# A DRAM-to-DRAM cast of two row tiles, issued per row tile instead of for both at once

## The chip, the core and the metric

The kernel runs on one core of a Trainium2 chip. The metric is the device time of one execution in microseconds (us). A core has TensorE (PE in the profile; PEld is its weight load), VectorE (DVE), ScalarE (ACT), GpSimd (POOL) and SyncE (SP), which work side by side and wait for each other through semaphores, and 16 DMA engines that move data when POOL or SP issues a transfer.

## The reference

```python
# a: 1024 x 4096 float32, b: 4096 x 4096 float32
x = np.matmul(a, b)
return special.logsumexp(x, axis=-1)      # 1024 values
```

## The kernel before

**Tiling.** Rows of `a` are split into 8 row tiles m of 128 (row p*8 + m stands in tile m), the inner dimension k into 32 tiles of 128, the columns of `b` into 8 blocks `nb` of 512. TensorE works in float16; the DMAs that POOL issues cast from float32 to float16 on the way. TensorE needs `a` transposed, and the tile `aT` holds it so for the whole run.

**Seven products instead of eight.** Two row tiles make a pair q (tiles 2q and 2q+1; q = 0 to 3), two k tiles a pair i (16 of them), and a block of 512 columns is two halves of 256. Each q and block is then a 2x2 block product, done with seven products m1 to m7 of 16 matmuls each (128x128 by 128x256) rather than eight. For that VectorE makes sums and differences: of `aT` the tiles `s1`, `s2`, `s5` (`a_sums_early`) and two differences in place (`a_sums_late`), and of each block of `b` the tiles T1, T4, T6 (in `tb`) and two more in place (`make`). The order of the products of one q is m1, m5, m2, m6, m3, m4, m7; ScalarE copies results out of PSUM between them, VectorE adds them up and takes row maxima, ScalarE sums exponentials.

**Stages.** In the first 65 us row tiles 0 to 5 come in, are transposed on TensorE and multiplied plainly with block 0. Then `plan` gives the steps: step 0 is block 1 with q = 0, 1, 2 worked jointly; steps 1 to 6 are blocks 2 to 7 with q = 0 to 3; the last two steps do q = 3 for blocks 0 and 1. PSUM tiles are named acc_q_h (h = 0 or 1, with a running number behind), so acc_2_0_1475 belongs to q = 2 of step 1 and acc_3_0_1608 to q = 3 of step 1. Columns of `b` are in tiles b_0 to b_3, one for each quarter of k, again with a running number: 744 to 747 are block 2 (used in step 1), 1205 to 1208 are block 3 (used in step 2).

**Row tiles 6 and 7** (q = 3) take another way, in step 0 (L356 to L365). For each half h of k (2048 columns), POOL issues a DMA that casts both row tiles from `a` to a float16 tile in DRAM, `a16_h` (2 x 128 x 2048; the profile names the two a_0_752 and a_1_756). Then SP issues two transposing DMAs from `a16_h` into `aT`, one for each row tile. VectorE makes the sums of q = 3 for the lower half of k behind q = 1 of step 1 (L529 to L531) and for the upper half in q = 2 of step 1, ahead of m3 (L503 to L505). q = 3 of step 1 is their first user.

**Order.** Each engine works its own instructions strictly in the order of the program (`manual_schedule`). POOL's order around the casts is: four loads of block 2, the casts, two loads of block 3, then a one-row copy into `ident` (L349) that reads what the first pair of transposes wrote and so holds POOL until they have landed, then the other two loads of block 3.

Of the kernel before, what the change touches and what calls it, by code (L numbers as in the profile page):

```python
# [13 lines left out]
def kernel(  # L14
# [6 lines left out]
    nc = tc.nc  # L21
# [12 lines left out]
    MT, KT, NB = M // P, K // P, N // FD  # L34
# [5 lines left out]
    a_m = a.rearrange("(p mt) k -> mt p k", mt=MT)  # L40
# [295 lines left out]
    for step, (_, qs) in enumerate(plan):  # L336
# [4 lines left out]
        if more:  # L341
            if plan[step + 1][0] is again1:
                nxt = last
            else:
                nxt = plan[step + 1][0]()
                if step == 1:
# [3 lines left out]
                        out=ident[0:1, 0:2], in_=aT[0:1, 0, 0, MP - 1, :, 0]  # L350
# [5 lines left out]
        if step == 0:  # L356
            KH = K // 2
            for h in range(2):
                a16 = dram_pool.tile([2, P, KH], f16, name=f"a16_{h}")
                nc.gpsimd.dma_start(out=a16, in_=a_m[MT - 2 :, :, ts(h, KH)])  # L360
                for m in range(2):
                    nc.sync.dma_start_transpose(
                        aT[:, ts(h, KP // 2), :, MP - 1, m, :].rearrange("p i t c -> p (i t) c"),
                        a16[m],
                    )  # L365
        quads = {}
        for q in qs:
# [91 lines left out]
            if final:  # L459
# [29 lines left out]
                    out=w, in_=w, func=AF.Exp, bias=n0, scale=-1.0, accum_out=l0  # L489
# [76 lines left out]
```

## Time and profile before

| | |
|---|---|
| runs | median 453.17 us of 6 (452.39 to 453.24) |
| profiled execution | 453.78 us, span of its instructions 451.9 us |
| PE busy | 417.0 us (92%) |
| DVE, ACT, POOL busy | 260.7 us, 109.1 us, 75.0 us |
| DMA | 52.99 MB written, mean 117 GB/s |
| q0 (issued by POOL), q1 (issued by SP) | 50.35 MB, 2.10 MB |

Times inside an execution are us from the start of its span. DMA bytes and GB/s count what is written, which for a casting load is half of what is read. The DMA share of a stretch is the mean busy share of the 16 DMA engines; it can be over 1 because an engine works on overlapping packets. "[22.40 <-ACT ...]" behind a row is the time that its engine sat idle before it and what ended that. A row with x16 merges 16 instructions of one kind. PEclk is the granted clock of TensorE, 1.00 being full.

### The profile page before, as it was taken

What the parts mean: (1) busy time and instruction counts of PE and PEld (TensorE: products, weight loads), DVE (VectorE), ACT (ScalarE), POOL (GpSimd) and SP (SyncE); (2) the same over time, 40 slices, a digit from 0 to 9 for tenths busy, and PEclk for the clock granted to TensorE, in tenths of its full rate; (3) what the DMA queues carried; (4) which work ended last, traced back from release to release, by engine and by line L of the source; (5) the groups of instructions that cost most, each with busy time, mean ns of one, the idle gap of its engine ahead of it and who ended that gap; (6) DMA issues with size and microseconds to landing.
All of it is one profiled execution on the core that took longest, in us unless ns stands there. A gap on an engine that the chain in (4) does not pass through costs nothing.

```text
span 451.9 us, 8525 instructions
## 1 busy us (share of the span) xinstructions
PE 417.0 (92%) x3647; PEld 350.0 (77%) x3647; DVE 260.7 (58%) x571; ACT 109.1 (24%) x278; POOL 75.0 (17%) x115
## 2 busy tenths in 40 slices
PE   7999999999990099999999999999999999999993
PEld 2555568888880078888888888888888888888882
DVE  1557687789220369634782269325953478264995
ACT  1222240242220002222222222212222222222214
POOL 7776752010000203000200003000300020020000
PEclk9999999999996579999999999999999999999997
DMA  8999999999229994950199009900594019899000
GB/s 120 202 202 203 202 206 207 207 160 185 57 55 73 174 177 77 207 91 1 17 207 151 1 1 154 208 14 1 85 207 83 0 19 207 150 187 188 0 2 0
DMA packets 61397, 52.99 MB, mean 117 GB/s; under 512 B 13744, under 2 KB 60848, under 8 KB 61360
## 3 DMA queue, kind: packets, MB, share of 16 engines
q0 software_dynamic: 52896, 50.35, 68.2%
q1 hardware_dynamic: 8464, 2.10, 4.7%
q8 instruction: 28, 0.46, 0.4%
q14 instruction: 9, 0.07, 0.0%
HBM read 100.66 MB, written 2.10 MB: 227 GB/s over the span
## 4 chain that ended last, share of the span: by engine, by line
PE 57%; another core or an unknown queue 30%; DVE 7%; DMA 4%; ACT 1%; issue 0%; SPq 0%; DVEq 0%; ACTq 0%
DMA aT<-a_0_752 4%; PE acc_3_0_1608 L378 2%; PE acc_1_0_4052 L378 2%; PE acc_2_0_3640 L378 2%; PE acc_3_0_3228 L378 2%; PE acc_1_0_2972 L378 2%; PE acc_2_0_2560 L378 2%; PE acc_3_0_2148 L378 2%; PE acc_0_0_1764 L378 2%; PE acc_3_0_3768 L378 2%; PE acc_0_0_2304 L378 2%; PE acc_2_0_4184 L378 2%; PE acc_0_0_3924 L378 2%; PE acc_1_0_3512 L378 2%; PE acc_0_0_3384 L378 2%
## 5 line engine op out<-in xcount | busy, mean ns | idle before, releaser
L378 PEld LDWEIGHTS <-aT 128*128 128x128 f16 x1856 | 182.3, 98 | 45.6 <-issue 23.8
L378 PEld LDWEIGHTS <-s_71 128*128 128x128 f16 x464 | 46.0, 99 | 6.2
L378 PEld LDWEIGHTS <-s_73 128*128 128x128 f16 x464 | 45.4, 98 | 5.3
L378 PEld LDWEIGHTS <-s_72 128*128 128x128 f16 x464 | 45.4, 98 | 5.3
L192 POOL DMA_DIRECT2D tb<-in_a_dram x48 | 26.0, 546 | 6.3 <-PE tps_97 L203 1.6
L81 DVE TENSOR_TENSOR s_71<-aT 128x256 f16<-128x256 f16 (+1 forms) x26 | 8.2, 316 | 32.6 <-DMA aT<-a_0_752 27.2
L203 PEld LDWEIGHTS <-tb 128*128 128x128 f16 x192 | 14.3, 99 | 16.0 <-DMA tb<-in_a_dram 7.6
L221 PEld LDWEIGHTS <-aT 128*128 128x128 f16 x192 | 16.8, 98 | 11.9 <-ACT aT L216 0.3
L216 ACT COPY aT<-tps_98 128x512 f16<-128x512 f16 x24 | 14.1, 586 | 43.9 <-PE tps_98 L203 43.9
L214 DVE COPY aT<-tps_97 128x512 f16<-128x512 f16 x24 | 10.2, 425 | 25.1 <-PE tps_97 L203 25.0
L378 PE MATMUL acc_2_0_1475<-b_0_744,aT 128*128 128x256 f16 x8 | 1.6, 339 | 22.4 <-ACT s_2_1477 L507 22.4
L84 DVE TENSOR_TENSOR aT<-aT 128x256 f16<-128x256 f16 (+1 forms) x56 | 16.2, 342 | 0.0
L203 PE MATMUL tps_97<-ident,tb 128*128 128x128 f16 x96 | 9.6, 223 | 1.9 <-DMA tb<-in_a_dram 1.9
L203 PE MATMUL tps_98<-ident,tb 128*128 128x128 f16 x96 | 9.3, 219 | 0.7 <-DMA tb<-in_a_dram 0.7
L349 POOL COPY ident<-aT 1x2 f16<-1x2 f16 x1 | 0.7, 667 | 53.6 <-DMA aT<-a_0_752 53.6
L138 POOL DMA_DIRECT2D b_0_3916<-in_b_dram x1 | 0.9, 881 | 45.4 <-PE acc_3_0_3768 L378 45.4
L138 POOL DMA_DIRECT2D b_0_3376<-in_b_dram x1 | 0.9, 881 | 45.4 <-PE acc_3_0_3228 L378 45.4
L138 POOL DMA_DIRECT2D b_0_2836<-in_b_dram x1 | 0.9, 881 | 45.4 <-PE acc_3_0_2688 L378 45.4
L138 POOL DMA_DIRECT2D b_0_2296<-in_b_dram x1 | 0.9, 890 | 45.1 <-PE acc_3_0_2148 L378 45.1
L81 DVE TENSOR_TENSOR s_72<-aT 128x256 f16<-128x256 f16 (+1 forms) x26 | 8.2, 316 | 0.0
L81 DVE TENSOR_TENSOR s_73<-aT 128x256 f16<-128x256 f16 (+1 forms) x26 | 8.2, 316 | 0.0
L282 PE MATMUL acc_1_96<-s_73 128*128 128x512 f16 x15 | 6.6, 581 | 1.2 <-DVE s_73 L285 1.2
(1047 smaller groups left out, 901.4 us busy)
## 6 DMA issues: line engine op xcount, KB each, us to landing
tb<-in_a_dram POOLq DMA_DIRECT2D x48, 128.0 KB, 5.9
aT<-in_b_dram POOLq DMA_DIRECT2D x4, 1024.0 KB, 15.1
b_0_83<-in_b_dram POOLq DMA_DIRECT2D x4, 256.0 KB, 6.1
b_1_84<-in_b_dram POOLq DMA_DIRECT2D x4, 256.0 KB, 6.2
b_2_85<-in_b_dram POOLq DMA_DIRECT2D x4, 256.0 KB, 6.2
b_3_86<-in_b_dram POOLq DMA_DIRECT2D x4, 256.0 KB, 6.2
b_0_87<-in_b_dram POOLq DMA_DIRECT2D x2, 512.0 KB, 8.6
b_1_88<-in_b_dram POOLq DMA_DIRECT2D x2, 512.0 KB, 11.8
```

The source lines that it names most:

```text
L81: nc.vector.tensor_tensor(out=o, in0=x, in1=y, op=ALU.add)
L84: nc.vector.tensor_tensor(out=o, in0=x, in1=y, op=ALU.subtract)
L138: nc.gpsimd.dma_start(out=self.raw[lo // GI][:, lo % GI : lo % GI + hi - lo], in_=b_rows[:, lo:hi, :, ts(self.nb, FD)],)
L192: nc.gpsimd.dma_start(out=slot, in_=a_m[m, :, k0 * P : (k0 + kn) * P])
L203: nc.tensor.matmul(pst[:, ts(j, P)], src[:, ts(j, P)], ident, is_transpose=True, start=(j == 0), stop=(j == kn - 1),)
L214: nc.vector.tensor_copy(out=dst, in_=v)
L216: nc.scalar.copy(out=dst, in_=v)
L221: nc.tensor.matmul(pt, aT[:, i, kp, m // 2, m % 2, :], blk0.raw[i // GI][:, i % GI, kp, :], start=(done[m] == 0), stop=(done[m] == KT - 1),)
L282: nc.tensor.matmul(acc[2][1], zeros[:, 0:P], zeros[:, 0:FD], start=True, stop=True)
L349: nc.gpsimd.tensor_copy(out=ident[0:1, 0:2], in_=aT[0:1, 0, 0, MP - 1, :, 0])
L378: nc.tensor.matmul(c, lhs(i), rhs(i), start=(start and i == 0), stop=(i == KP - 1), skip_group_check=True,)
```

## The change

The one DMA of POOL for each k half, which casts both row tiles, becomes two, one for each row tile. The first dimension of the source was the row tile (2); it is now the row (128). The bytes, the DRAM tiles, the four transposes and everything else stay.

```diff
             for h in range(2):
                 a16 = dram_pool.tile([2, P, KH], f16, name=f"a16_{h}")
-                nc.gpsimd.dma_start(out=a16, in_=a_m[MT - 2 :, :, ts(h, KH)])
+                for m in range(2):
+                    nc.gpsimd.dma_start(out=a16[m], in_=a_m[MT - 2 + m, :, ts(h, KH)])
                 for m in range(2):
                     nc.sync.dma_start_transpose(
```

On POOL, around the casts, this stands in a row before (DMASW0 to DMASW7 are the eight semaphores that POOL's DMAs take in turn, DMAHW0 and DMAHW1 those of the first two transposes):

```order
L138 DMA b_2_746<-in_b_dram 128x8x512 [waits DMASW2_49,PE_49]
L138 DMA b_3_747<-in_b_dram 128x8x512 [waits DMASW3_49,PE_49]
L360 DMA a_0_752<-in_a_dram 256x1x2048 [waits DMASW4_49]
L360 DMA a_1_756<-in_a_dram 256x1x2048 [waits DMASW5_49]
L138 DMA b_0_1205<-in_b_dram 128x8x512 [waits DMASW6_49,DVE_49,PE_49]
L138 DMA b_1_1206<-in_b_dram 128x8x512 [waits DMASW7_49,DVE_49,PE_49]
L349 COPY ident<-aT 1x2 [waits DMAHW1_49,DMAHW0_49,Pool_49]
L138 DMA b_2_1207<-in_b_dram 128x8x512 [waits DMASW0_49,DVE_49,PE_49]
L138 DMA b_3_1208<-in_b_dram 128x8x512 [waits DMASW1_49,DVE_49,PE_49]
```

After the change, at the same place on POOL (the running numbers of later tiles go up by one or two):

```order
L138 DMA b_2_746<-in_b_dram 128x8x512 [waits DMASW2_49,PE_49]
L138 DMA b_3_747<-in_b_dram 128x8x512 [waits DMASW3_49,PE_49]
L361 DMA a_0_752<-in_a_dram 128x2048 [waits DMASW4_49]
L361 DMA a_0_752<-in_a_dram 128x2048 [waits DMASW5_49]
L361 DMA a_1_757<-in_a_dram 128x2048 [waits DMASW6_49]
L361 DMA a_1_757<-in_a_dram 128x2048 [waits DMASW7_49]
L138 DMA b_0_1207<-in_b_dram 128x8x512 [waits DMASW0_49,DVE_49,PE_49]
L138 DMA b_1_1208<-in_b_dram 128x8x512 [waits DMASW1_49,DVE_49,PE_49]
L349 COPY ident<-aT 1x2 [waits DMAHW1_49,DMAHW0_49,Pool_49]
L138 DMA b_2_1209<-in_b_dram 128x8x512 [waits DMASW2_49,DVE_49,PE_49]
L138 DMA b_3_1210<-in_b_dram 128x8x512 [waits DMASW3_49,DVE_49,PE_49]
```

Two casts became four; what follows stands two semaphores further on, and the order of the rest is the same.

On SP, which does nothing before the first transpose, stood before:

```order
L362 DMA_TRANSPOSE aT_70<-a16_0_752 128x16x128 [waits DMASW4_49]
L362 DMA_TRANSPOSE aT_70<-a16_0_752 128x16x128
L362 DMA_TRANSPOSE aT_70<-a16_1_756 128x16x128 [waits DMASW5_49]
L362 DMA_TRANSPOSE aT_70<-a16_1_756 128x16x128
L535 DMA out_0_dram<-lg_80 128x8 [waits DVE_49]
```

And now:

```order
L363 DMA_TRANSPOSE aT_70<-a16_0_752 128x16x128 [waits DMASW4_49]
L363 DMA_TRANSPOSE aT_70<-a16_0_752 128x16x128 [waits DMASW5_49]
L363 DMA_TRANSPOSE aT_70<-a16_1_757 128x16x128 [waits DMASW6_49]
L363 DMA_TRANSPOSE aT_70<-a16_1_757 128x16x128 [waits DMASW7_49]
L536 DMA out_0_dram<-lg_80 128x8 [waits DVE_49]
```

Each transpose now waits for the cast of its own row tile alone. PE, DVE and ACT have the same instructions in the same order.

## The prediction

> **What bounds the kernel now.** I read the slices of the page first, then the blocks of TensorE in time, then what each engine waited for around the one hole. The page's busy rows, in 40 slices of 11.3 us:
>
> ```profile
> PE   7999999999990099999999999999999999999993
> PEclk9999999999996579999999999999999999999997
> ```
>
> PE is full but for two empty slices (136 to 158 us), and the granted clock dips there. In PE's timeline (start, length; 16 matmuls a row):
>
> ```profile
> 112.85 1.91 PE L378 MATMUL acc_1_0_1342<-tb,s_71 128*128 128x256 f16 x16
> 125.08 1.91 PE L378 MATMUL acc_2_0_1475<-tb,s_71 128*128 128x256 f16 x16
> 133.81 1.91 PE L378 MATMUL acc_2_1_1476<-tb,aT 128*128 128x256 f16 x16
> 158.12 1.01 PE L378 MATMUL acc_2_0_1475<-b_0_744,aT 128*128 128x256 f16 x4 [22.40 <-ACT s_2_1477 L507]
> 161.49 3.12 PE L378 MATMUL acc_3_0_1608<-tb,s_71 128*128 128x256 f16 x16
> 174.93 1.91 PE L378 MATMUL acc_0_0_1764<-tb,s_71 128*128 128x256 f16 x16
> ```
>
> A block of seven products takes 125.08 - 112.85 = 12.23 us when nothing stops it, 1.75 us a product. The block of q = 2 in step 1 takes 161.49 - 125.08 = 36.41, the next one 13.44. In the first, m7 waits 22.40 us for a ScalarE copy, and then runs at half clock. Who held ScalarE:
>
> ```profile
> 157.70 0.37 ACT L507 COPY s_2_1477<-acc_2_0_1475 128x256 f32<-128x256 f32 x1 [23.71 <-DVE s_2_1477 L81]
> 126.26 0.69 DVE L87 TENSOR_REDUCE negmax<-acc_1_0_1342 128x1 f32<-128x512 f32 x1
> 154.17 0.69 DVE L81 TENSOR_TENSOR s_71<-aT 128x1024 f16<-128x1024 f16 x1 [27.22 <-DMA aT<-a_0_752]
> 157.19 0.42 DVE L81 TENSOR_TENSOR s_2_1477<-s_2_1477 128x256 f32<-128x256 f32 x1
> 161.16 0.69 DVE L81 TENSOR_TENSOR s_71<-aT 128x1024 f16<-128x1024 f16 x1 [3.09 <-DMA aT<-a_1_756]
> 138.01 16.07 DMA aT<-a_0_752
> SPq L362 <- DMA a_0_752<-in_a_dram: 135.9, 1, 135.9
> 136.56 14.84 SPq L362 DMA_TRANSPOSE aT<-a_0_752  x2
> ```
>
> VectorE is free at 126.95, but the sums of q = 3 stand next in its row and need the first pair of transposes, which lands at 154.08 (138.01 + 16.07, chain of waits). The add that ScalarE needs stands behind them. SP could start transposing only at 136.56, when the first cast had landed. So the chain is cast, transpose, VectorE, ScalarE, PE, and the cast is its long link. POOL's issues, and the DMA list (KB each, us to landing):
>
> ```profile
> 69.16 0.88 POOL L138 DMA_DIRECT2D b_3_747<-in_b_dram  x1 [1.65 <-DMA b_1_88<-in_b_dram]
> 71.42 1.09 POOL L360 DMA_DIRECT2D a_0_752<-in_a_dram  x1 [1.38 <-DMA b_2_89<-in_b_dram]
> 98.81 0.93 POOL L138 DMA_DIRECT2D b_0_1205<-in_b_dram  x1 [23.77 <-PE acc_2_0_764 L378]
> 99.73 0.90 POOL L138 DMA_DIRECT2D b_1_1206<-in_b_dram  x1
> ...
> b_3_90<-in_b_dram POOLq DMA_DIRECT2D x2, 512.0 KB, 19.1
> b_3_747<-in_b_dram POOLq DMA_DIRECT2D x1, 1024.0 KB, 30.2
> a_0_752<-in_a_dram POOLq DMA_DIRECT2D x1, 1024.0 KB, 65.1
> a_1_756<-in_a_dram POOLq DMA_DIRECT2D x1, 1024.0 KB, 64.5
> ```
>
> Stretches (length, busy times, then PE clock, DMA share, GB/s written):
>
> ```profile
> 80.00:84.00 4.00, 4.00 (x40) 3.58 (x38) 3.56 (x10) 1.45 (x3) 0.00 (x0) 1.00 1.24 207
> 104.00:108.00 4.00, 4.00 (x39) 3.57 (x38) 4.00 (x7) 0.37 (x1) 0.00 (x0) 1.00 1.19 208
> 116.00:120.00 4.00, 4.00 (x39) 3.59 (x38) 0.00 (x0) 0.59 (x1) 0.00 (x0) 1.00 0.26 53
> 128.00:132.00 4.00, 4.00 (x39) 3.59 (x38) 0.00 (x0) 0.59 (x1) 0.00 (x0) 1.00 0.26 53
> 156.00:158.00 2.00, 0.00 (x0) 0.00 (x0) 1.97 (x5) 0.30 (x2) 0.60 (x1) 0.50 1.19 239
> ```
>
> With all engines at work 207 GB/s are written. While only the casts are left it is 53 GB/s at a share of 0.26: four of sixteen engines, two for each cast. Each of these four is as fast as ever (53/4 = 13.3 GB/s against 207/16 = 12.9); twelve are idle.
>
> **The change part by part.** *The casts.* Everything ahead of them in the queue is unchanged, so they begin when b_3_747 is done, at 69.16 + 30.2 = 99.4 us. The four write 2.10 MB in all; on 16 engines at 207 GB/s that is 10.1 us, done at 109.5.
>
> *What shares the engines now.* b_0 and b_1 of block 3, issued at 98.81 and 99.7, queue behind the casts on every engine: 2.10 MB, 10.1 us. The first pair of transposes (1.05 MB) runs beside all this, from about 103.4: one cast (2.5) behind 99.4, and the 1.45 from SP's start to the first transpose's (136.56 to 138.01). Alone it goes at 239 GB/s (156 to 158 us, mostly transposes), 4.4 us. Sum: 99.4 + 10.1 + 10.1 + 4.4 = 124.0. Mixing costs something: before, the pair took 16.07 us beside the rest of the same two loads on four engines (0.52 MB at 53 GB/s, 9.9 us, plus 4.4 gives 14.3), so 1.8 were lost. I add that: the first pair lands at 125.8, not 154.08.
>
> *How late it may be.* VectorE reaches it at 126.95. From landing to m7's restart are 158.12 - 154.08 = 4.04 us, and m7's own turn is 125.08 + 6 x 1.75 = 135.55, so up to 131.5 PE feels nothing. The second pair was used 161.16 - 154.08 = 7.08 after the first, its first sum done 0.69 later; PE needs it half a product into q = 3, at 137.31 + 0.87 = 138.2, so 130.4. The L349 copy, which holds POOL until the first pair has landed, frees b_2 and b_3 of block 3:
>
> ```profile
> 154.24 0.67 POOL L349 COPY ident<-aT 1x2 f16<-1x2 f16 x1 [53.61 <-DMA aT<-a_0_752]
> 170.36 0.69 DVE L81 TENSOR_TENSOR tb<-b_3_1208 128x1024 f16<-128x1024 f16 x1 [1.38 <-DMA b_3_1208<-in_b_dram]
> 171.63 0.37 ACT L507 COPY s_3_1610<-acc_3_0_1608 128x256 f32<-128x256 f32 x1
> ```
>
> b_3 was used 16.3 us after the first pair's landing; its sum (0.6), the add behind it (0.42), the L507 copy (0.37) and 0.1 of handover must be through before m7 of q = 3, at 137.31 + 10.48 = 147.8, so 130.0. That is the tightest: 4.2 us of cover over 125.8, and from there on each us late costs one.
>
> *The gain.* Both blocks go back to 12.23: 36.41 - 12.23 = 24.18, and 174.93 - 161.49 - 12.23 = 1.21, which is q = 3's share of the half clock; together 25.4 us. Behind 174.93 everything is paced by PE and moves up as it stands.
>
> *Costs.* POOL issues two more DMAs, at most 1.09 us each. The last two wait for the two b_3_90 loads to land:
>
> ```profile
> 58.35 1.51 POOL L138 DMA_DIRECT2D b_3_90<-in_b_dram  x2
> 63.81 0.88 POOL L138 DMA_DIRECT2D b_1_745<-in_b_dram  x1
> ...
> b_1_745<-in_b_dram POOLq DMA_DIRECT2D x1, 1024.0 KB, 25.4
> ```
>
> The second was issued at about 59.1 and landed by 59.1 + 19.1 = 78.2. POOL is done by 79.3 plus one issue, 80.4, and its next instruction waited for PE until 98.81 anyway: nothing, with 18 us of cover; without it b_0 of block 3 would slip. The two loads behind now wait for b_0_744 and b_1_745, the later of which landed at 63.81 + 25.4 = 89.2, ahead of 98.81: nothing. SP's two added waits let a transpose start earlier, never later. DVE's upper sums now come close behind its lower ones, in idle time. A stage at 207 GB/s between 99 and 124 in place of 53 touches no one: nothing that arrives there is used before 126.95.
>
> The profiled execution then takes 453.78 - 25.4 = 428.4 us. It lay 0.6 above the median, so the runs: 453.17 - 25.4 = 427.8 us.
>
> **The rivals.**
>
> *The casts are slower on 16 engines than four times four.* They read and write DRAM; the load stretches only read it. At 104 to 108 us the loads and casts together read 416 GB/s and wrote 53 to DRAM with no loss (208 written in all). Casts on all engines ask for 414 and 207, 621 in all. If 469 were the ceiling, they take 13.4 us, the pair lands at 129.1, and nothing is lost; if DRAM-to-DRAM goes at 207 each way, they take 20.3 us, the pair lands at 136.0, and 6.0 us are lost: 433.8. For it: no row shows more than 469. Against: one engine casting to DRAM loses nothing beside one that loads. In between, 431. The Trainium skill ("DMA: Bandwidth & Descriptors", Latency and other measured facts, the row on HBM row pitch) gives 207 to 214 GB/s per direction for copies between HBM tensors at best; by that the upper end, 433.8, would hold. No row here shows such a copy on all engines, so I give it 15 in 100 together with what lies between.
>
> *Transposes suffer more beside busy engines.* The 1.8 us lost came with four engines loading:
>
> ```profile
> 142.00:150.00 8.00, 0.00 (x0) 0.00 (x0) 0.00 (x0) 0.00 (x0) 0.00 (x0) 0.50 1.30 78
> ```
>
> 78 GB/s at a share of 1.30 says that all engines were held up by those four. With four times the load beside it the loss could be 7.2: the pair lands at 131.2, 1.2 us are lost, 429.0; if the second pair suffers as well, 431. 10 in 100.
>
> *The new transfers don't spread.* If a cast of 128 rows still went to two engines or fewer, everything stays: 453.2. For it: no row shows a DRAM-to-DRAM transfer on 16. Against: the other transfers of POOL have 128 partitions first and keep all engines busy. 5 in 100. The Trainium skill (same page, Why a DMA increments its semaphore by 16 and not by 1) states that a transfer runs on the largest number up to 16 that divides the first size of both sides: 2 before, 16 now; by it this rival is out.
>
> *Slower.* The 53 GB/s are a limit of casting into DRAM, not of the four engines. Then the casts take 39.5 us still, but now block every engine, with b_0 and b_1 of block 3 behind them: 99.4 + 39.5 + 10.1 + 4.4 + 1.8 = 155.2, 1.1 us later than before: 454.3, and more if spreading costs. It decides from a rate under 2.10/38.4 = 54.7 GB/s on, where the pair passes 154.08. Against: 13.3 GB/s per engine is just an engine's rate in loads. 3 in 100.
>
> **How the numbers follow.** 67 in 100 stay for the forecast, 427.8 us, whose own range is 427.0 to 428.8 (the spread of the runs and 0.4 for the modelled ends of matmuls). The two partial cases, 25 in 100, lie from 428.5 to 434; up to 432.5 the range takes in most of them: 427.0 to 432.5. A measurement here tells 0.2% (0.9 us) from no change. Faster: 67 + 15 + 10 = 92 in 100. Within 0.2%: 5, the transfers that don't spread. Slower: 3.
>
> **What the changed profile would show.** Right: casts landing some 30 to 38 us after their issue instead of 65; no stretch at 53 GB/s between 112 and 136, but 200 or so from 99 to about 120; SP's first transpose at 102 to 106; DVE's wait for aT<-a_0 gone or under 3 us; no half clock in the middle; q = 2 and q = 3 of step 1 at 12.2 us each; POOL's L349 at about 126. Wrong: a first pair landing behind 130, with a wait of DVE for aT or for b_3 of block 3 in q = 3 of step 1, or a share of 0.26 again.

## The result and the profile after

| | before | after |
|---|---|---|
| median | 453.25 us (20 runs, 452.39 to 454.2) | 428.45 us (10 runs, 428.12 to 429.56) |
| ratio after to before | | 0.9455, 95% interval 0.9447 to 0.9464 |
| profiled execution, its span | 453.78 us, 451.9 us | 428.54 us, 426.8 us |
| PE busy | 92% | 97% |

The change makes the kernel 5.5% faster. The forecast was 427.8 us (range 427.0 to 432.5). On the page of the changed kernel the hole in PE and the dip of its clock are gone:

```profile
PE   6999999999999999999999999999999999999992
PEclk9999999999999999999999999999999999999998
```

PE's timeline, at the places shown of before:

```profile
125.15 1.91 PE L379 MATMUL acc_2_0_1477<-tb,s_71 128*128 128x256 f16 x16
135.63 0.60 PE L379 MATMUL acc_2_0_1477<-b_0_744,aT 128*128 128x256 f16 x4
137.37 1.91 PE L379 MATMUL acc_3_0_1610<-tb,s_71 128*128 128x256 f16 x16
149.60 1.91 PE L379 MATMUL acc_0_0_1766<-tb,s_71 128*128 128x256 f16 x16
```

Both blocks take 12.22 and 12.23 us (before 36.41 and 13.44); m7 starts at 135.63 with nothing idle ahead of it. The chain that had held it, in the order in which it now runs (POOL's issues, the list of DMAs, SP, POOL's waiting copy, VectorE):

```profile
71.00 0.55 POOL L361 DMA_DIRECT2D a_0_752<-in_a_dram  x1 [1.42 <-DMA b_2_89<-in_b_dram]
78.63 0.52 POOL L361 DMA_DIRECT2D a_1_757<-in_a_dram  x1 [1.81 <-DMA b_3_90<-in_b_dram]
a_0_752<-in_a_dram POOLq DMA_DIRECT2D x2, 512.0 KB, 30.0
a_1_757<-in_a_dram POOLq DMA_DIRECT2D x2, 512.0 KB, 29.9
101.09 21.23 SPq L363 DMA_TRANSPOSE aT<-a_0_752  x2
125.12 0.17 POOL L349 COPY ident<-aT 1x2 f16<-1x2 f16 x1 [24.46 <-DMA aT<-a_0_752]
126.94 0.68 DVE L81 TENSOR_TENSOR s_71<-aT 128x1024 f16<-128x1024 f16 x1
141.28 0.69 DVE L81 TENSOR_TENSOR tb<-b_3_1210 128x1024 f16<-128x1024 f16 x1
```

The first cast lands at 101.0 (71.00 + 30.0), the last at 108.5 (78.63 + 29.9); before, the two landed at 136.5 and 138.5. The first pair of transposes is there at 125.1 instead of 154.1, and VectorE comes to its sums at 126.94 without a wait; b_3 of block 3 is there when its sum is due. The stretches that show it (length, busy times, PE clock, DMA share, GB/s written):

```profile
100.00:104.00 4.00, 4.00 (x39) 3.58 (x38) 4.00 (x8) 0.53 (x1) 0.66 (x1) 1.00 1.06 214
104.00:108.00 4.00, 4.00 (x39) 3.58 (x37) 4.00 (x7) 0.42 (x2) 0.00 (x0) 1.00 1.07 203
116.00:120.00 4.00, 4.00 (x39) 3.59 (x37) 0.00 (x0) 0.58 (x1) 0.00 (x0) 1.00 1.32 158
```

While the casts run (100 to 108 us) the DMA share is 1.06 to 1.07 and 203 to 214 GB/s are written; until 104 no transpose moves data yet, so the 214 are the casts' own. The stretch from 116 to 120, where there were 53, has 158; transposes and loads now run in it side by side.

### The profile page after: what moved, and what is told of

Same layout as the page of the kernel before. It is cut to its first block, busy times and chain, and to the rows that moved or that the text cites. A ratio compares the mean times of both kernels' runs of the same rounds, so it can differ in the third digit from the quotient of the medians.

```text
span 426.8 us, 8527 instructions
## 1 busy us (share of the span) xinstructions
PE 412.7 (97%) x3647; PEld 348.5 (82%) x3647; DVE 260.5 (61%) x571; ACT 109.0 (26%) x278; POOL 74.3 (17%) x117
## 4 chain that ended last, share of the span: by engine, by line
PE 80%; DVE 10%; DMA 5%; POOL 2%; ACT 2%; issue 1%; DVEq 0%; ACTq 0%; POOLq 0%
DMA tb<-in_a_dram 5%; PE acc_2_0_766 L379 2%; PE acc_3_0_2690 L379 2%; PE acc_0_0_3926 L379 2%; PE acc_2_0_3102 L379 2%; PE acc_1_0_3514 L379 2%; PE acc_0_0_3386 L379 2%; PE acc_0_0_2306 L379 2%; PE acc_3_0_2150 L379 2%; PE acc_2_0_2022 L379 2%; PE acc_3_0_1610 L379 2%; PE acc_1_0_4054 L379 2%; PE acc_2_0_3642 L379 2%; PE acc_3_0_3230 L379 2%; PE acc_1_0_2974 L379 2%; PE acc_0_0_2846 L379 2%
## 5 line engine op out<-in xcount | busy, mean ns | idle before, releaser
L214 DVE COPY aT<-tps_97 128x512 f16<-128x512 f16 x24 | 10.2, 425 | 25.1 <-PE tps_97 L203 25.0
L138 POOL DMA_DIRECT2D aT<-in_b_dram x4 | 3.5, 899 | 21.2 <-PE acc_1_0_4054 L379 21.2
L282 PE MATMUL acc_1_96<-s_73 128*128 128x512 f16 x15 | 5.4, 486 | 1.2 <-DVE s_73 L285 1.2
L81 DVE TENSOR_TENSOR tb<-aT 128x1024 f16<-128x1024 f16 x8 | 5.0, 686 | 0.0
```

The costliest lines, as they stand in the source:

```text
L81: nc.vector.tensor_tensor(out=o, in0=x, in1=y, op=ALU.add)
L138: nc.gpsimd.dma_start(out=self.raw[lo // GI][:, lo % GI : lo % GI + hi - lo], in_=b_rows[:, lo:hi, :, ts(self.nb, FD)],)
L214: nc.vector.tensor_copy(out=dst, in_=v)
L282: nc.tensor.matmul(acc[2][1], zeros[:, 0:P], zeros[:, 0:FD], start=True, stop=True)
```

## The experiments

The theory: only the number of engines that work on a cast matters, and PE pays for nothing but how late the first pair of transposes lands behind 130.0 us. The main rival: the gain comes from four transfers in place of two, and from each transpose waiting for its own row tile alone. The diffs below are excerpts, against the kernel after the change. Landings are those of each kernel's profiled execution.

**One transfer for each half, rows first.**

```diff
-                for m in range(2):
-                    nc.gpsimd.dma_start(out=a16[m], in_=a_m[MT - 2 + m, :, ts(h, KH)])
+                nc.gpsimd.dma_start(
+                    out=a16.rearrange("m p k -> p m k"),
+                    in_=a_m[MT - 2 :, :, ts(h, KH)].rearrange("m p k -> p m k"),
+                )
```

> One cast for each k half, as before the change, but with the row as first dimension (128, then the row tile 2) on both sides. Spread theory (only the number of DMA engines matters): both casts run on 16 engines, the first pair of transposes lands at about 125, and the time is the changed kernel's, 428.5 us. Split theory (the gain comes from four separate transfers and a wait of each transpose for its own row tile): as before, 453 us.

Measured: 428.33 us, ratio to before 0.9447 (0.9431 to 0.9463). POOL's waiting copy in its timeline:

```profile
125.44 0.18 POOL L349 COPY ident<-aT 1x2 f16<-1x2 f16 x1 [25.19 <-DMA aT<-a]
```

Two transfers in place of four, and the first pair lands at 125.4, against 125.1. The whole gain is there without the split, so the rival falls: the order of the dimensions decides.

**Four transfers, two engines each.**

```diff
-                    nc.gpsimd.dma_start(out=a16[m], in_=a_m[MT - 2 + m, :, ts(h, KH)])
+                    nc.gpsimd.dma_start(
+                        out=a16[m].rearrange("(r s) k -> s r k", s=2),
+                        in_=a_m[MT - 2 + m, :, ts(h, KH)].rearrange("(r s) k -> s r k", s=2),
+                    )
```

> Four casts, one for each row tile and k half, as in the changed kernel, but with a first dimension of 2 (even and odd rows). Spread theory: two engines each, eight in all, 106 GB/s; the casts end at about 119, the first pair of transposes lands at 135 to 136, 5 to 6 us behind the 130.0 up to which there is cover: 433.5 to 434.5 us. Split theory: the changed kernel's time, 428.5 us.

Measured: 436.0 us, ratio 0.9617 (0.9598 to 0.9635). A stretch of the casts, VectorE's first sum and PE's m7:

```profile
120.00:124.00 4.00, 4.00 (x40) 3.59 (x37) 1.23 (x3) 2.19 (x7) 0.00 (x0) 1.00 1.00 109
136.55 1.90 DVE L81 TENSOR_TENSOR s<-aT 128x1024 f16<-128x1024 f16 x3 [9.91 <-DMA aT<-a]
140.50 3.41 PE L382 MATMUL acc<-b,aT 128*128 128x256 f16 x16 [5.09 <-ACT s L511]
```

The split alone does not do it. The pair lands 0.5 us later than the later end of what was expected. The time is 1.5 us over the expectation, which left out the half clock: PE idles for 5.09 us, and m7 then takes 3.41 us, 1.50 more than the usual 1.91.

**One half only.** Two kernels: the lower half of k spread and the upper not, and the other way round (h == 1).

```diff
-                for m in range(2):
-                    nc.gpsimd.dma_start(out=a16[m], in_=a_m[MT - 2 + m, :, ts(h, KH)])
+                if h == 0:
+                    for m in range(2):
+                        nc.gpsimd.dma_start(out=a16[m], in_=a_m[MT - 2 + m, :, ts(h, KH)])
+                else:
+                    nc.gpsimd.dma_start(out=a16, in_=a_m[MT - 2 :, :, ts(h, KH)])
```

> The lower k half is cast in two transfers of 128 rows, the upper half in one as before. If engines only share bandwidth: the first pair lands at 115 to 120, the second pair waits for a cast on two engines (to 144) and comes at about 150: 441 to 444 us. If each engine takes one packet of either queue in turn, and a transpose ends with its slowest engine: the two engines that cast the upper half to about 144, and then load block 3, hold the first pair until about 158: about 458 us, slower than before.

> The upper k half is cast in two transfers of 128 rows, the lower half in one as before. If engines only share bandwidth: the lower cast lands at about 137, the first pair at 143 to 146 with little left to compete: 441 to 444 us. If each engine takes one packet of either queue in turn: on the two slow engines the upper casts and the two loads of block 3 are still to come, and the first pair lands at 156 to 159: 455 to 459 us, slower than before.

Measured: lower only 459.49 us, ratio 1.0123 (1.0101 to 1.0145); upper only 457.77 us, ratio 1.0095 (1.0077 to 1.0112). Of the lower-only kernel a stretch, SP and VectorE's first sum, then of the upper-only kernel the same three:

```profile
116.00:120.00 4.00, 4.00 (x39) 3.58 (x37) 0.00 (x0) 0.80 (x2) 0.00 (x0) 1.00 1.47 80
100.93 61.41 SPq L366 DMA_TRANSPOSE aT<-a  x4
160.55 1.89 DVE L81 TENSOR_TENSOR s<-aT 128x1024 f16<-128x1024 f16 x3 [33.85 <-DMA aT<-a]
```

```profile
116.00:120.00 4.00, 4.00 (x39) 3.60 (x37) 0.25 (x1) 1.14 (x3) 0.00 (x0) 1.00 0.13 27
136.94 23.46 SPq L366 DMA_TRANSPOSE aT<-a  x4
158.22 1.89 DVE L81 TENSOR_TENSOR s<-aT 128x1024 f16<-128x1024 f16 x3 [31.96 <-DMA aT<-a]
```

Each half of the change by itself makes the kernel slower than before, by 1.2% and 1.0%. In the upper-only kernel two engines alone write 27 GB/s until 137, with the spread casts of the upper half behind them. In the lower-only kernel transposing starts at 101 and yet the first pair lands at 160.5. Its stretch shows that not only two engines are late: a share of 1.47 at only 80 GB/s can't come from two, so packets stand in the others too. Before, the same loads beside casts on four engines, with no transpose running, went at 208 GB/s and a share of 1.19 (104 to 108). How many packets each queue finished in four microseconds (packets, MB, share; q0 holds loads and casts, q1 the transposes), first in the lower-only kernel (116 to 120), then in the changed kernel (112 to 116: loads and transposes alone), then before (142 to 146: loads on four engines only):

```profile
q0 software_dynamic: 197, 0.27, 86.1%
q1 hardware_dynamic: 198, 0.05, 61.2%
```

```profile
q0 software_dynamic: 624, 0.62, 91.6%
q1 hardware_dynamic: 623, 0.16, 30.4%
```

```profile
q1 hardware_dynamic: 627, 0.16, 107.3%
q0 software_dynamic: 156, 0.16, 22.9%
```

Where both queues have work on every engine, they finish one packet each in turn (624 and 623). Before, with loads on four engines only, there were four packets of transposes to one of loads: 627 on 16 engines are 39 each, 156 on four are also 39. So the twelve engines without loads went no faster than the four with them. In the lower-only kernel a transpose gets 198 packets through where the changed kernel gets 623. Two engines that write 27 GB/s (the upper-only stretch) finish some 13 rows of 4 KB each in 4 us, and 198 packets are 12.4 for each of 16 engines: about one packet of a transpose, on every engine, for each row that the two slow engines cast. No view names single engines, so that all engines keep step is worked out from these counts. The expectations' even sharing of bandwidth would have given 441 to 444; both times came out where one packet of each queue in turn puts them.

**How late the first pair may be.** Two kernels with more casts of 128 rows ahead of the four (n = 2 and n = 4), whose data nobody reads.

```diff
             KH = K // 2
+            for j in range(n):
+                x16 = dram_pool.tile([P, KH], f16, name=f"x16_{j}")
+                nc.gpsimd.dma_start(out=x16, in_=a_m[j, :, 0:KH])
             for h in range(2):
```

> The changed kernel with two more casts of 128 rows (1.05 MB, nobody reads them) ahead of the four: everything behind comes 5.05 us later. Cover as worked out (up to a landing of the first pair at 130.0): it lands at about 130.2, and the time stays 428.5 to 428.8 us. If each us behind 126.94, where VectorE reaches the sums, costs one: 431.8 us.

> The changed kernel with four more casts of 128 rows (2.10 MB, nobody reads them) ahead of the four: everything behind comes 10.1 us later. Cover as worked out: the first pair lands at about 135.2, 5.2 us behind the cover: 433.7 us, and up to 1.5 more if the wait of PE is long enough for half clock. If each us behind 126.94 costs one: 436.8 us and more.

Measured: 430.49 us with two, ratio 0.9506 (0.9479 to 0.9533); 434.28 us with four, 0.9584 (0.957 to 0.9598). VectorE's first sum and PE's rows with a wait (with four, also the product behind the first wait), with two more casts and then with four:

```profile
131.29 1.90 DVE L81 TENSOR_TENSOR s<-aT 128x1024 f16<-128x1024 f16 x3 [4.53 <-DMA aT<-a]
138.61 1.05 PE L382 MATMUL acc<-tb,s 128*128 128x256 f16 x8 [0.46 <-DVE s L81]
161.61 1.91 PE L382 MATMUL acc<-b,aT 128*128 128x256 f16 x16 [0.98 <-ACT s L511]
```

```profile
135.25 1.90 DVE L81 TENSOR_TENSOR s<-aT 128x1024 f16<-128x1024 f16 x3 [8.80 <-DMA aT<-a]
139.20 2.96 PE L382 MATMUL acc<-b,aT 128*128 128x256 f16 x16 [3.98 <-ACT s L511]
141.95 2.57 PE L382 MATMUL acc<-tb,s 128*128 128x256 f16 x16
166.36 1.91 PE L382 MATMUL acc<-b,aT 128*128 128x256 f16 x16 [0.89 <-ACT s L511]
```

With two, the pair lands at 131.3 and not at 130.2, so it is 1.3 past the cover; PE waits 0.46 us in the middle of the first product of q = 3 and 0.98 ahead of m7 of q = 0 in step 2, together 1.44, and the median rises by 2.0. That lies between the two times expected, 428.5 to 428.8 and 431.8, so both were missed. With four the pair is 5.3 past; PE waits 3.98 ahead of m7 of q = 2 and 0.89 ahead of m7 of q = 0 in step 2, and the two products behind the first wait take 1.05 and 0.66 longer. That is 6.6 in all; PE had come to q = 2 some 0.6 us sooner than in the changed kernel (124.57 against 125.15), and the median rises by 5.8. VectorE itself waited 4.53 and 8.80, so not every microsecond behind 126.94 costs; behind 130 each one costs about one.

**The loads beside the transposes.** POOL's waiting copy ahead of all four loads of block 3, and (not shown) no such copy at all:

```diff
+                    nc.gpsimd.tensor_copy(
+                        out=ident[0:1, 0:2], in_=aT[0:1, 0, 0, MP - 1, :, 0]
+                    )
                     nxt.load(0, GI)
                     nxt.load(GI, 2 * GI)
-                    nc.gpsimd.tensor_copy(
-                        out=ident[0:1, 0:2], in_=aT[0:1, 0, 0, MP - 1, :, 0]
-                    )
```

> The changed kernel with POOL's waiting copy moved ahead of all four loads of block 3, so that no load runs beside the first pair of transposes. If the loads are what makes the pair slow: it lands at 113 to 115 instead of 125, the four loads come behind it and block 3 is complete at about 139, in time for its use at 141.3; the time stays 428.5 us. If the pair is slow for another reason: it lands as in the changed kernel, the loads begin at 125, block 3 is complete at 147, and 2 to 3 us are lost.

> The changed kernel without POOL's waiting copy: all four loads of block 3 stand in the queue when the first pair of transposes starts. If each engine takes one packet of either queue in turn: nearly the whole pair runs packet by packet beside loads and lands at about 134, 431 to 432 us. If engines share bandwidth evenly or the transposes are hardly touched: the pair lands by 126 to 130, 428.5 us.

Measured: copy first 428.71 us, ratio 0.9464 (0.9446 to 0.9483); no copy 435.67 us, ratio 0.9605 (0.9581 to 0.9628). Of the first, POOL's copy and the sums of block 3; of the second, VectorE's first sum and PE's m7:

```profile
114.69 0.17 POOL L347 COPY ident<-aT 1x2 f16<-1x2 f16 x1 [35.00 <-DMA aT<-a]
139.17 2.49 DVE L81 TENSOR_TENSOR tb<-b 128x1024 f16<-128x1024 f16 x4
```

```profile
135.70 1.90 DVE L81 TENSOR_TENSOR s<-aT 128x1024 f16<-128x1024 f16 x3 [9.01 <-DMA aT<-a]
139.65 3.22 PE L376 MATMUL acc<-b,aT 128*128 128x256 f16 x16 [4.19 <-ACT s L505]
```

With no load beside it the pair lands at 114.7, with two at 125.1, with four at 135.7: each two loads (2.10 MB, 10.1 us at 207 GB/s) cost the pair 10.4 to 10.6 us, their whole time. With the copy first the time stays, though the pair lands 10.4 us earlier: nothing was waiting for it any more. Nor is there 10 us more to spare. All four loads of block 3 are now issued behind the pair, and between 138 and 142 us 73 GB/s are written where the changed kernel writes 75; the loads end at the same time, and it was the last of them that set the 130.0. Without the copy the pair lands 1.7 us later than expected and PE idles long enough for half clock; the time is 3.7 us above the expected 432. The profiled execution of that kernel took 433.82 us at a granted clock of 0.993, the least of its four runs (others 435.57 to 435.97 at 0.986 to 0.987), so the median holds some 2 us that this trace does not show. The lower clock of those runs would fit more time at half clock; that is not shown.

**The next wait.** In the changed kernel one wait of PE is left between the load phase and the end, m7 in q = 0 of step 1 (list of waits):

```profile
PE acc_0_0_1216 L379 <- ACT s_0_1218 L508: 0.8, 1, 0.8
```

```diff
+            if joint and tail:
+                held = [(r1, 2 * q + 1, nb), (r0, 2 * q, nb)]
+                continue
             if tail:
                 lse_max(r1, 2 * q + 1, nb)
             lse_max(r0, 2 * q, nb)
+            if step == 1 and q == 0:
+                for r, m, n in held:
+                    lse_max(r, m, n)
+                    lse_exp(r, m, n)
```

> The changed kernel with the row maxima (VectorE, 1.2 us) and exponentials of step 0's last q moved behind q = 0 of step 1. If the 0.80 us wait of PE ahead of m7 in q = 0 of step 1, the only one left in the middle of the changed kernel, comes from VectorE being late there: the wait goes and the time falls by 0.8 to 1.0 us against the changed kernel on the same chip (about 427.5 us). If another chain is just as late: no difference that can be measured.

> The changed kernel once more, on the same chip as the kernel with the later maxima, to compare with it: 428.4 us, 0.945 of the kernel before.

Measured: 427.29 us (426.91 to 427.41), ratio 0.9428 (0.9415 to 0.9441); the changed kernel beside it 428.09 us (427.95 to 428.75), ratio 0.945 (0.9437 to 0.9463). PE's waits in the kernel with the later maxima are these two, both in the first stage:

```profile
PE tps L203 <- DMA tb<-in_a_dram: 3.7, 4, 1.4
PE acc L282 <- DVE s L285: 1.2, 1, 1.2
```

The wait is gone, and the time falls by the 0.8 us of it. The two ranges of runs do not meet, though the intervals of the ratios overlap a little. This is the fastest version found.

## Why the prediction was right

All landings, on one scale (us). "Lost" is the median over 428.45:

| kernel | first pair lands | past 130.0 | lost |
|---|---|---|---|
| copy first | 114.7 | 0 | 0.3 |
| changed | 125.1 | 0 | 0 |
| one transfer, rows first | 125.4 | 0 | -0.1 |
| two more casts | 131.3 | 1.3 | 2.0 |
| four more casts | 135.3 | 5.3 | 5.8 |
| no copy | 135.7 | 5.7 | 7.2 |
| two engines each | 136.5 | 6.5 | 7.6 |
| before | 154.1 | 24.1 | 24.8 |
| upper only | 158.2 | 28.2 | 29.3 |
| lower only | 160.5 | 30.5 | 31.0 |

The 130.0 was worked out for the changed kernel's order on POOL; for "copy first" and "no copy", where the loads of block 3 are issued at other times, it is only a mark on the scale.

- *The chain.* Cast, transpose, VectorE, ScalarE, PE: right. The loss follows the landing of the first pair in every kernel (the first three differ by no more than the runs do), and past 130.0 a microsecond costs one, plus 0.5 to 1.5 us in all; where half clock follows, it is part of that.
- *The casts' own time.* Foreseen done at 109.5; the last landed at 108.5. Right, and the engines kept their rate. The first cast landed at 101.0, so SP began at 101.09, a little ahead of the 102 to 106 foreseen.
- *The landing.* Foreseen at 125.8, measured 125.1. That the pair pays the loads' full time is right (10.4 us for the two loads, by the run with the waiting copy first). The sum without the 1.8 for mixing, 124.0, was 1.1 short, with it 0.7 long. From the casts' real end, 108.5 + 10.1 + 4.4 = 123.0, so 2.1 us were lost; the term had about the right size. It is not all mixing with loads, as the prediction had it: with the copy first the last cast landed at about 109.2 (issued at 79.17, 30.0 us), no load ran beside the pair, and it came at 114.7, still 1.1 behind 109.2 + 4.4. Where that 1.1 comes from stays open.
- *The cover.* Foreseen up to 130.0; 125.1 and 125.4 lose nothing, 131.3 loses 1.44 us of PE. Right in size, within what two points 6 us apart can tell, and in part by luck: the wait that was to set it, m7 of q = 3 behind b_3, shows in neither kernel with more casts. What showed were the two looser limits, the first product of q = 3 (130.4 foreseen; 0.46 us of wait at 131.3) and m7 of q = 2 (131.5 foreseen; 3.98 us at 135.3), and 0.98 and 0.89 us at m7 of q = 0 in step 2, a wait that the prediction did not have: the loss does not end with q = 3.
- *The gain.* Foreseen 25.4 us, and 428.4 for the profiled execution; it took 428.54. The two blocks gave 25.40 of it (36.41 + 13.44 before, 12.22 + 12.23 after). Span fell by 25.1, the medians by 24.8. The 0.65 us between 427.8 and 428.45 come mostly from the anchor: the profiled execution lay 0.6 above the median before, and only 0.1 after.
- *The rivals.* DRAM as a ceiling: out; the casts alone wrote 214 GB/s while reading twice that. The Trainium skill ("DMA: Bandwidth & Descriptors", Latency and other measured facts) gives a rate of 207 to 214 GB/s per direction for copies between HBM tensors. The reads here went at twice 214, so it is no limit on them. Transposes that suffer more: out in the changed kernel; beyond the loads' own time the pair lost 2.1 us, where this rival had 7.2. Transfers that do not spread: out. *Slower*, a limit of casting into DRAM: out by the same 214. A slower kernel turned up all the same, from a cause that the prediction did not name: in the kernels with one half only, a transpose ran beside two engines that still cast.

What was argued and not tried by itself: why a first dimension of 2 leads to two engines, and that it is two, since no view counts engines; the number is read from the rates. All orders tried fit one rule, the number of engines being the largest up to 16 that divides the first dimension of both sides (2 first: 53 GB/s for two transfers, 27 for one, 109 for four; 128 first: 203 to 214). The old cast's destination stands as 256 rows in POOL's row before (256x1x2048), so by this rule it was the source's 2 that counted. First dimensions between 2 and 128 were not tried. The Trainium skill (same page, Why a DMA increments its semaphore by 16 and not by 1) states that rule for the first dimension of both sides, and these runs agree with it.

## What to carry to other kernels

Look at the DMA share of a stretch, not of the run: a quarter of the full rate at a quarter of the share meant here that most engines had no part in the transfer, and putting the dimension with 128 rows outermost on both sides cured it, in one transfer or in several. Treat a DMA transpose that uses all engines as going at the pace of the slowest of them: here, as long as two still held a long backlog, starting it earlier gained nothing, and curing only half of the backlog cost 1%. Work out how late a landing may be before PE feels it, and look for the few microseconds of PE's idleness that bring half clock on top.

## What the runs showed of the hardware that was not expected

- A transfer on two engines comes with many more small packets. The page's line on DMA packets, before, with one transfer rows first (two transfers each), then for the changed kernel and with two engines each (four transfers each):

```profile
DMA packets 61397, 52.99 MB, mean 117 GB/s; under 512 B 13744, under 2 KB 60848, under 8 KB 61360
DMA packets 57813, 52.97 MB, mean 124 GB/s; under 512 B 10160, under 2 KB 57264, under 8 KB 57776
DMA packets 57845, 52.97 MB, mean 124 GB/s; under 512 B 10192, under 2 KB 57296, under 8 KB 57808
DMA packets 61429, 52.99 MB, mean 122 GB/s; under 512 B 13776, under 2 KB 60880, under 8 KB 61392
```

  With equal numbers of transfers, two engines in place of 16 mean 3584 more packets under 512 bytes both times: 2 x 14 idle engines x 128 rows for each busy one, and 4 x 14 x 64. That they belong to the idle engines is an inference from the count.
- Half clock sets in after short idleness: behind waits of PE of 3.98, 4.19 and 5.09 us the next product took 2.96, 3.22 and 3.41 us in place of 1.91 (granted clock 0.65 from 139 to 142 us with four more casts, 0.50 from 139 to 142 with no copy and from 141 to 143 with two engines each); behind a wait of 0.98 us it took 1.91.
- A DMA transpose beside ordinary transfers goes packet by packet with them (624 and 623 packets in 4 us), and a backlog on two engines held it on all (198 packets in 4 us).
